# A hybrid decoder layer on one core: weight casts, sums and matmuls chained in stream order, and half a hidden block deferred

## The chip, the cores and the metric

The kernel runs on one core of one Trainium2 chip. The metric is the device time of one execution in microseconds (us); lower is better. A profile is one execution recorded by the hardware profiler.

## The reference

One decoder layer in fp32, 256 tokens, width 2048. Batch and depth are 1. Cut to what matters:

```python
def reference(x, mem, ...):
    hn = rmsnorm(x, norm_mix_w)
    q, k, v, g_ret, xr, yr, g_a, g_b = jnp.split(hn @ w_in, offsets, axis=-1)
    ret = head_groupnorm(chunkwise_retention(rotary(q), rotary(k), v))   # 8 heads, chunks of 128
    hr = rg_lru(causal_dwconv(xr, ...), ...)                             # gated linear recurrence
    merged = (jax.nn.sigmoid(g_a) * ((jax.nn.silu(g_ret) * ret) @ w_proj_ret)
              + jax.nn.sigmoid(g_b) * ((jax.nn.gelu(yr) * hr) @ w_proj_rnn))
    h = x + merged @ w_mix_out
    h = h + memory_cross_attention(rmsnorm(h, norm_xa_w), rmsnorm(mem, norm_mem_w), ...)  # 4 heads
    up = causal_dwconv(rmsnorm(h, norm_ffn_w) @ ffn_w_up, ...)           # 2048 -> 2 x 5632, 3 taps
    gate, val = jnp.split(up, 2, axis=-1)
    h = h + (jax.nn.silu(gate) * val) @ ffn_w_down                       # 5632 -> 2048
    return rmsnorm(h, final_norm_w)
```

## The kernel before, in words

All large weights come as one stream of pieces of 1 MB, `raw`, 128 partitions by 4 k-tiles by 512 columns (`wall`). Every piece is one unit of work. `prefetch(n)` keeps `AHEAD` = 2 units ready: SyncE's queue loads the piece (some pieces are added to an earlier one by an accumulating transfer in GpSimd's queue), ScalarE casts it to a short mantissa (`hi`, L284), and VectorE takes the difference (`lo = raw - hi`, L285). TensorE then multiplies with both, the activations being split the same way, so that fp32 accuracy is kept: in `gemm_t` (L349) the weight is the stationary operand, a 512-wide matmul with `hi` and a 256-wide one with `lo`; in `upper_n` (L360, L361) and `lower_n` (L367) the activations are stationary. There are `RAW_BUFS` = 5 buffers for pieces and `PART_BUFS` = 3 each for `hi` and `lo`.

Products whose two column blocks are done together (`pair_products`) use seven instead of eight block products for the first eight k-tiles, with sums of weight blocks, and plain products for k-tiles 8 to 15. `PAIR_UNITS` gives the order of the eleven units: products q1 to q7 with 12 matmuls each and four plain units p with 24 each. A weight block A, B or C stays in its buffer: after q5 VectorE adds B to A's buffer (L292), after q6 it adds C (L290), and the accumulating transfer changes B and A.

`later(n, fn)` puts a step off until n more units are done. The other work (rotary, scores and decay of the retention, group norm, recurrence, cross-attention, convolution) is written between the units like this, and the order on each engine comes from a list scheduler that works with priorities; results of a pair are read with raised priority. So the program's order need not be the order on an engine.

The FFN goes in three parts of 4, 4 and 3 hidden blocks of 512 (`FF_PARTS`). For each block `conv_up` makes the gate and the value half, two accumulators of two tiles each (`pr` = 0, 1): the product, `scaled` (two VectorE steps per accumulator, L541 and L672), a convolution step on ScalarE (L1187) and four taps on VectorE (L1189). Then come tanh (L1257), two VectorE steps (L1258, L1259) and the split into high and low (L551 on ScalarE, L552 on VectorE). `hid` holds eight such tile pairs per part. In parts 0 and 1 the down projection goes as two paired products (`pair_add`, which adds to the residual rows, L427); in the last part, as plain ones (`down`).

In the retention, a head's scores (`sc`) are multiplied by the decay matrix into a tile `pret` (L768, L769), then split into `ps` (L771 on ScalarE, L772 on VectorE). After the fourth head of a group `normalise` computes a reciprocal root (L610 on GpSimd, L796) and scales. In the value pair, results are copied and subtracted into `o` (L454, L460, L470).

Of the kernel before, what the change touches and what calls it, by code (L numbers as in the profile page):

```python
# [13 lines left out]
ALU = mybir.AluOpType  # L14
# [16 lines left out]
RAW_BUFS = 5  # L31
# [63 lines left out]
def residual_plan(w):  # L95
# [8 lines left out]
    ("p", None, (1, 8)),  # L104
    ("q3", "B", ("new", 1, 1)),
    ("p", None, (1, 12)),
# [3 lines left out]
    ("p", None, (0, 8)),  # L110
    ("q7", "B", ("add", 0, 1)),
    ("q4", "A", ("sum",)),
    ("p", None, (0, 12)),
]

def entry_units(e):

    w, row, nk, cols = e[0], e[1], e[2], e[3:5]
    if len(cols) == 1:
        return [("p", None, "new", (w, tuple(row + (k + i) * P for i in range(KC)), cols[0])) for k in range(0, nk, KC)]  # L120
    out = []
    for kind, slot, a in PAIR_UNITS:
        if kind == "p":
# [29 lines left out]
def hybrid_layer(  # L153
# [20 lines left out]
    bp = ctx.enter_context(tc.tile_pool(name="bp", bufs=25))  # L174
# [58 lines left out]
    held, after = {}, []  # L233
# [12 lines left out]
    def prefetch(n):  # L246
        while len(ahead) < n and taken[0] < len(stream):
# [30 lines left out]
            for a, b in pieces:  # L278
                if taken[0] <= 4:
                    xs[2 * (taken[0] - 1) + (b - 1) // KH]  # L280
                if first and b <= KH:
                    dve.tensor_copy(hi[:, a:b], raw[:, a:b])  # L282
                else:
                    act.copy(hi[:, a:b], raw[:, a:b])  # L284
                dve.tensor_tensor(  # L285
                    out=lo[:, a:b], in0=raw[:, a:b], in1=hi[:, a:b].bitcast(F32), op=ALU.subtract
                )
            if after:
                to, by = (held[i] for i in after.pop())
                dve.tensor_tensor(out=to, in0=to, in1=by, op=ALU.add)  # L290
            if kind == "q5":
                dve.tensor_tensor(out=raw, in0=raw, in1=held["B"], op=ALU.add)  # L292
# [33 lines left out]
    def gemm_t(w, row, st, nk, col):  # L326
# [4 lines left out]
        for k0, parts in chunks(nk, w, row, col):  # L331
# [9 lines left out]
            for i, run in enumerate(runs):  # L341
                for t, pr, kk, j in run:
# [6 lines left out]
                    pe.matmul(  # L349
                        a, part, sx, start=k == 0 and t == 0, stop=k == nk - 1 and t == 0, skip_group_check=True  # L350
                    )
# [4 lines left out]
    def upper_n(o, ops, parts, start):  # L356

        for kk, (h, l) in enumerate(ops):
            hi = parts[kk // KH][0][:, kk % KH, :]
            pe.matmul(o, h, hi, start=start and kk == 0, stop=False, skip_group_check=True)  # L360
            pe.matmul(o, l, hi, start=False, stop=False, skip_group_check=True)  # L361

    def lower_n(o, ops, parts, stop):

        for kk, (h, _) in enumerate(ops):
            lo = parts[kk // KH][1][:, kk % KH, :]
            pe.matmul(o, h, lo, start=False, stop=stop and kk == KC - 1, skip_group_check=True)  # L367
# [15 lines left out]
    def pair_products(w, row, st, ss, c0, c1, out):  # L383
# [7 lines left out]
        begun, plain = set(), 0  # L391
# [10 lines left out]
        for kind, parts in units(*e):  # L402
            if kind == "p":
                k0 = 8 + 4 * (plain % 2)
                run(
                    (((r, "r"), (w_, "w")), ((y, "y"), (u, "u")))[plain // 2],
                    [
                        [halves(st[(k0 + k) // 2], k % 2, slice(tt * P, (tt + 1) * P)) for k in range(KC)]
                        for tt in range(2)
                    ],  # L410
                    parts,
                )
                plain += 1
# [7 lines left out]
            with tc.high_priority(URGENT):  # L421
                out(f"p{plain}" if kind == "p" else kind, x, z, yu, rw)

    def pair_add(w, row, st, ss, c0, c1, h0, h1):
# [4 lines left out]
        def out(kind, x, z, yu, rw):  # L429
# [10 lines left out]
            elif kind == "p4":  # L440
# [4 lines left out]
    def pair_out(w, st, ss, c0, r=None):  # L445
# [30 lines left out]
        def out(kind, x, z, yu, rw):  # L476
# [11 lines left out]
            elif kind == "p4":  # L488
# [267 lines left out]
    def retain(g, qr, kr, vs, dec, gates):  # L756
# [4 lines left out]
        def scores(hh):  # L761
# [5 lines left out]
            pr_ = tp.tile([P, 384], F32, tag="pret", bufs=2, name=nm("pret"))  # L767
# [7 lines left out]
        def values(hh, phi, plo):  # L775
# [405 lines left out]
    def conv_up(c0, b, dst):  # L1181
        for pr, a in enumerate(gemm_t("ffn_w_up", 0, h2s, NT, c0 + b * BW)):
            z = scaled(a, "uz")
            for j in range(2):
                t = c0 // P + 4 * b + 2 * pr + j
                y = dst[:, 2 * pr + j, :]
                act.activation(y, z[:, j, :], AF.Identity, scale=pf[:, 2, t : t + 1], bias=pf[:, 3, t : t + 1])  # L1187
                for s in range(1, 3):
                    dve.scalar_tensor_tensor(  # L1189
                        out=y[:, s:S], in0=z[:, j, 0 : S - s], scalar=pf[:, 2 - s, t : t + 1], in1=y[:, s:S],  # L1190
                        op0=ALU.mult, op1=ALU.add,
                    )
# [52 lines left out]

    b0 = 0
    for part, nb_ in enumerate(FF_PARTS):
        final = part == len(FF_PARTS) - 1
        hid, hid_sums = [], []
        for b in range(b0, b0 + nb_):  # L1250
            gt, vl = big([P, 4, S], s="fg"), big([P, 4, S], s="fv")
            conv_up(0, b, gt)
            conv_up(FF, b, vl)
            for pr in range(2):
                cs = slice(2 * pr, 2 * pr + 2)
                th, o = tmp("ft"), tmp("fo")
                act.activation(th, gt[:, cs, :], AF.Tanh, scale=0.5)  # L1257
                dve.scalar_tensor_tensor(out=o, in0=th, scalar=1.0, in1=gt[:, cs, :], op0=ALU.add, op1=ALU.mult)  # L1258
                dve.tensor_tensor(out=o, in0=o, in1=vl[:, cs, :], op=ALU.mult)  # L1259
                hid.append(split_pair(o, 0.5))  # L1260
                if nb_ == 4 and len(hid_sums) < KC:
                    hid_sums.append(sums(o, 0.5))
# [51 lines left out]
```

## Time and profile before

| | |
|---|---|
| time, median of 3 runs | 2009.64 us (2009.12 to 2011.54) |
| the profiled execution | 2011.54 us, span 2009.8 us, mean granted clock 0.998 |
| TensorE busy | 1989.9 us, 99% of the span |
| VectorE busy | 1585.2 us, 79% |
| ScalarE busy | 1158.7 us, 58% |
| data moved | 430.97 MB, mean 214 GB/s |

Engines are PE (TensorE), PEld (its weight loads), DVE (VectorE), ACT (ScalarE), POOL (GpSimd) and SP (SyncE, which issues most transfers). In the timeline a line gives the start, the duration, the engine, the line of the kernel, the operation and its tiles; in square brackets stands the idle time just before, and what ended it. Matmuls are pipelined: the distance from start to start tells what one costs, not its duration.

### The profile page before, as it was taken

To read this page: it belongs to the slowest core of one execution; us is meant where nothing else is said; L and a number is where in the kernel's file an instruction comes from. 1 tells how busy PE (TensorE), PEld (TensorE's weight loads), DVE (VectorE), ACT (ScalarE), POOL (GpSimd) and SP (SyncE) were. 2 spreads that over 40 slices of the span, in tenths; PEclk is the share of its full clock that TensorE was granted. 3 is DMA by queue.
4 is the path that set the end of the run, shared out by engine and by line. 5 is a ranking of instruction groups with operands and counts; after the bars stand their busy time and mean duration, and the time that the engine had idled before them with its cause. 6 is when DMAs were issued, how large, how long until landed. Compare 5 with 4: busy or idle time off the path is not lost.

```text
span 2009.8 us, 24882 instructions
## 1 busy us (share of the span) xinstructions
PE 1989.9 (99%) x10072; PEld 1691.7 (84%) x10072; DVE 1585.2 (79%) x1588; ACT 1158.7 (58%) x1167; POOL 43.0 (2%) x52
## 2 busy tenths in 40 slices
PE   9999999999999999999999999999999999999998
PEld 7888888888888888888888888888878888788887
DVE  6798797889985886768888768777787787886765
ACT  6565656767665554566766556555544555544552
POOL 0000000000000000000000000000000000000000
PEclk9999999999999999999999999999999999999999
DMA  9664674655977775877886647655567555584552
GB/s 369 237 226 140 229 245 176 210 202 145 295 245 246 214 246 189 262 249 234 267 246 204 254 130 223 233 187 196 182 197 238 194 189 188 170 264 173 200 198 84
DMA packets 76003, 430.97 MB, mean 214 GB/s; under 512 B 8304, under 2 KB 13040, under 8 KB 28144
## 3 DMA queue, kind: packets, MB, share of 16 engines
q1 hardware_dynamic: 68608, 384.81, 52.2%
q0 software_dynamic: 5760, 41.95, 11.5%
q10 hardware_dynamic: 1520, 2.63, 0.4%
q8 instruction: 79, 1.29, 0.2%
q14 instruction: 36, 0.29, 0.0%
HBM read 418.87 MB, written 10.49 MB: 214 GB/s over the span
## 4 chain that ended last, share of the span: by engine, by line
PE 91%; DVE 5%; DMA 1%; issue 1%; ACT 1%; POOL 0%; SPq 0%; POOLq 0%; ACTq 0%; DVEq 0%
PE acc L349 37%; PE acc L360 17%; PE acc L361 17%; PE acc L367 16%; DVE lo L285 2%; PE sm L518 2%; DMA raw<-in_wall 1%; PE sm L530 1%; ACT hi L284 1%; PE acc L518 1%; PE sm L892 1%; DVE raw L292 0%; DVE fv L1189 0%; DVE tb L718 0%; DMA xt<-in_mem_t 0%
## 5 line engine op out<-in xcount | busy, mean ns | idle before, releaser
L285 DVE TENSOR_TENSOR lo<-raw,hi 128x2048 fp32r<-128x2048 f32 (+1 forms) x420 | 950.7, 2268 | 299.1 <-ACT hi L284 286.0
L284 ACT CAST hi<-raw 128x2048 fp32r<-128x2048 f32 (+1 forms) x418 | 792.8, 1902 | 624.1 <-PE acc L361 292.6
L360 PE MATMUL acc<-hi,s 128*128 128x512 f32 x1336 | 523.3, 392 | 4.3 <-ACT hi L284 3.9
L361 PE MATMUL acc<-hi,s 128*128 128x512 f32 x1336 | 520.7, 390 | 0.2 <-DVE s L575 0.2
L349 PE MATMUL acc<-s,hi 128*128 128x512 f32 x2176 | 518.0, 391 | 2.2 <-DVE hi L282 1.1
L349 PEld LDWEIGHTS acc<-s,hi 128*128 128x128 f32 x2176 | 401.9, 188 | 82.1 <-ACT hi L284 1.8
L367 PE MATMUL acc<-lo,s 128*128 128x512 f32 x1336 | 340.1, 392 | 0.1
L360 PEld LDWEIGHTS acc<-hi,s 128*128 128x128 f32 x1336 | 251.0, 188 | 58.0 <-ACT hi L284 5.2
L367 PEld LDWEIGHTS acc<-lo,s 128*128 128x128 f32 x1336 | 250.1, 188 | 53.6 <-DVE lo L285 0.5
L361 PEld LDWEIGHTS acc<-hi,s 128*128 128x128 f32 x1336 | 251.0, 188 | 52.2 <-DVE s L575 1.0
L349 PEld LDWEIGHTS acc<-s,lo 128*128 128x128 f32 x2176 | 277.0, 191 | 9.9 <-DVE lo L285 1.3
L349 PE MATMUL acc<-s,lo 128*128 128x256 f32 x2176 | 282.9, 283 | 0.5 <-DVE lo L285 0.5
L360 PE MATMUL acc<-hi,ss 128*128 128x512 f32 x320 | 127.2, 397 | 3.6 <-DVE o L470 1.7
L361 PE MATMUL acc<-hi,ss 128*128 128x512 f32 x320 | 125.5, 392 | 0.0
L367 PE MATMUL acc<-lo,ss 128*128 128x512 f32 x320 | 86.0, 390 | 0.0
L540 ACT COPY c<-acc 128x512 f32<-128x512 f32 x68 | 39.2, 578 | 75.2 <-PE acc L349 74.9
L360 PEld LDWEIGHTS acc<-hi,ss 128*128 128x128 f32 x320 | 60.6, 189 | 18.2 <-ACT hi L284 2.5
L361 PEld LDWEIGHTS acc<-hi,ss 128*128 128x128 f32 x320 | 60.6, 189 | 12.2
L367 PEld LDWEIGHTS acc<-lo,ss 128*128 128x128 f32 x320 | 60.0, 188 | 12.7
L265 POOL DMA_DIRECT2D raw<-in_wall x40 | 35.2, 879 | 1574.2 <-DVE lo L285 845.2
L427 DVE TENSOR_TENSOR nat<-nat,acc 128x512 f32<-128x512 f32 (+1 forms) x49 | 44.0, 910 | 6.7 <-PE acc L367 6.7
L290 DVE TENSOR_TENSOR raw<-raw,raw 128x2048 f32<-128x2048 f32 x20 | 45.8, 2288 | 0.4
(233 smaller groups left out, 1242.6 us busy)
## 6 DMA issues: line engine op xcount, KB each, us to landing
raw<-in_wall SPq DMA_DIRECT2D x333, 1024.0 KB, 4.9
raw<-in_wall POOLq DMA_DIRECT2D x40, 1024.0 KB, 8.0
xt<-in_x_t SPq DMA_DIRECT2D x11, 256.0 KB, 7.0
raw<-in_wall SPq DMA_DIRECT2D x5, 512.0 KB, 8.5
nat<-in_x ACTq DMA_DIRECT2D x4, 512.0 KB, 9.8
ret<-hd SPq DMA_DIRECT2D x8, 256.0 KB, 5.1
rnn<-rn SPq DMA_DIRECT2D x8, 256.0 KB, 3.1
kt<-ret SPq DMA_DIRECT2D x8, 256.0 KB, 5.6
```

The lines of the kernel that those rows point to most:

```text
L265: pool.dma_start(out=raw, in_=src, accum_op=ALU.add)
L284: act.copy(hi[:, a:b], raw[:, a:b])
L285: dve.tensor_tensor(out=lo[:, a:b], in0=raw[:, a:b], in1=hi[:, a:b].bitcast(F32), op=ALU.subtract)
L290: dve.tensor_tensor(out=to, in0=to, in1=by, op=ALU.add)
L349: pe.matmul(a, part, sx, start=k == 0 and t == 0, stop=k == nk - 1 and t == 0, skip_group_check=True)
L360: pe.matmul(o, h, hi, start=start and kk == 0, stop=False, skip_group_check=True)
L361: pe.matmul(o, l, hi, start=False, stop=False, skip_group_check=True)
L367: pe.matmul(o, h, lo, start=False, stop=stop and kk == KC - 1, skip_group_check=True)
L427: dve.tensor_tensor(out=o, in0=o, in1=i, op=op)
L518: pe.matmul(o, a, b, start=start and i == 0, stop=stop and i == 2, skip_group_check=True)
L530: pe.transpose(t[:, j, tt * P : (tt + 1) * P], rows[:, tt, k + j * P : k + (j + 1) * P], ident)
L540: act.copy(c, a[:, :, S:BW])
```

## The change

Five things change.

1. `in_turn` ties instructions of one queue to one another by scheduling edges without a semaphore: ScalarE's casts of weights in the stream's order, VectorE's casts, differences and weight sums, and TensorE's matmuls with weights. Each stays behind the one before it in the program.
2. The plain units are named and reordered: k-tiles 8 to 11 of both column blocks come first (p0, p1), k-tiles 12 to 15 later (p2, p3, the 8th and 11th unit). Before, the second plain unit (the 4th unit) took k-tiles 12 to 15.
3. The reciprocal root of the group norm is a step of its own, one unit after the fourth head, and `normalise` comes one unit later; `pret` shares the tag `tmp`.
4. In parts 0 and 1 of the FFN the value half of the last block is put off: convolution, gating and split of `pr` = 0 come after the first unit of the down projection, those of `pr` = 1 after the third.
5. The residual rows lie in memory (`fkept`) during the up projections: 12 stores and 12 loads of 512 KB in SyncE's queue. There is one more buffer for pieces (6) and one large buffer less (24).

The numbers of instructions on TensorE, ScalarE, VectorE and GpSimd stay as they were.

```diff
-RAW_BUFS = 5
+RAW_BUFS = 6
...
 PAIR_UNITS = [
     ("q1", "A", ("new", 0, 0)),
-    ("p", None, (1, 8)),
+    ("p0", None, (1, 8)),
     ("q3", "B", ("new", 1, 1)),
-    ("p", None, (1, 12)),
+    ("p1", None, (0, 8)),
     ("q5", "A", ("add", 0, 1)),
     ("q2", "C", ("new", 1, 0)),
     ("q6", "A", ("sum",)),
-    ("p", None, (0, 8)),
+    ("p2", None, (1, 12)),
     ("q7", "B", ("add", 0, 1)),
     ("q4", "A", ("sum",)),
-    ("p", None, (0, 12)),
+    ("p3", None, (0, 12)),
 ]
...
-    bp = ctx.enter_context(tc.tile_pool(name="bp", bufs=25))
+    bp = ctx.enter_context(tc.tile_pool(name="bp", bufs=24))
...
+    def in_turn(queue, ins):
+
+        if queue in last:
+            info = mybir.DependencyInfo(mybir.DependencyClass.NoSync, mybir.DependencyReason.DATA)
+            tc.add_manual_dep(ins.ins, last[queue].ins.name, info, reason="in turn")
+        last[queue] = ins
+        return ins
...
-                    act.copy(hi[:, a:b], raw[:, a:b])
-                dve.tensor_tensor(
+                    in_turn("a", act.copy(hi[:, a:b], raw[:, a:b]))
+                in_turn("d", dve.tensor_tensor(
                     out=lo[:, a:b], in0=raw[:, a:b], in1=hi[:, a:b].bitcast(F32), op=ALU.subtract
-                )
+                ))
...
-                    pe.matmul(
+                    in_turn("p", pe.matmul(
                         a, part, sx, start=k == 0 and t == 0, stop=k == nk - 1 and t == 0, skip_group_check=True
-                    )
+                    ))
...
             if hh == 3:
-                later(2, normalise)
-
-        def normalise():
+                later(1, rsqrt)
+
+        def rsqrt():
             rstd = rsqrt_small(stats[:, :, 1], 8, 1.0, GN_EPS).rearrange("p (h t) -> p h t", t=2)
+            later(1, lambda: normalise(rstd))
+
+        def normalise(rstd):
...
+    def put_rows(n, bs):
+        for b in bs:
+            sp.dma_start(out=fkept[n, b], in_=hrow[b])
+
+    def get_rows(n, bs):
+        for b in bs:
+            hrow[b] = big([P, 2, BW], s="nat")
+            sp.dma_start(out=hrow[b], in_=fkept[n, b])
...
+    put_rows(0, range(4))
...
+            for pr, z in enumerate(up(0, b)):
+                conv(0, b, pr, z, gt)
+            if b + 1 == b0 + nb_:
+                later(0, lambda part=part, n=2 if paired else 4: get_rows(part % 2, range(n)))
+            for pr, z in enumerate(up(FF, b)):
+                def finish_up(b=b, pr=pr, z=z, gt=gt, vl=vl, paired=paired):
+                    conv(FF, b, pr, z, vl)
+                    hidden(gt, vl, pr, paired)
+
+                if paired and b + 1 == b0 + nb_:
+                    later(1 + 2 * pr, finish_up)
+                else:
+                    finish_up()
...
             for b in (0, 2):
+                if b == 0:
+                    later(4, lambda part=part: get_rows(part % 2, (2, 3)))
                 pair_add("ffn_w_down", b0 * BW, hid, hid_sums, b * BW, (b + 1) * BW, hrow[b], hrow[b + 1])
+                put_rows((part + 1) % 2, (b, b + 1))
```

`conv` and `hidden` hold what stood in `conv_up` and in the loop over `pr`; the weight sums, `upper_n` and `lower_n` are wrapped in `in_turn` in the same way ("d" and "p").

More of the change, by code (lines that the diff above doesn't have):

```diff
@@ L366, in lower_n @@
             lo = parts[kk // KH][1][:, kk % KH, :]
[L367 removed]
+            in_turn("p", pe.matmul(o, h, lo, start=False, stop=stop and kk == KC - 1, skip_group_check=True))
     def gemm_n(w, row, st, nk, col):
@@ L402, in pair_products @@
         for kind, parts in units(*e):
[L403 to L413, printed above, removed]
+            if kind in rows:
+                k0, *to = rows[kind]
+                ops = [
+                    [halves(st[(k0 + k) // 2], k % 2, slice(tt * P, (tt + 1) * P)) for k in range(KC)]
+                    for tt in range(2)
+                ]
+                run(to, ops, parts)
             else:
```

72 lines of the change are left out of this document (37 added, 35 removed).

## The prediction

> **What bounds the kernel now.** I read the page's busy times and costliest groups first, then the table of stretches by 100 us, then the list of what TensorE waits for (us in total, times, longest), and last the timeline of the few places where that list has an entry.
>
> ```profile
> span 2009.8 us, 24882 instructions
> PE 1989.9 (99%) x10072; PEld 1691.7 (84%) x10072; DVE 1585.2 (79%) x1588; ACT 1158.7 (58%) x1167; POOL 43.0 (2%) x52
> L285 DVE TENSOR_TENSOR lo<-raw,hi 128x2048 fp32r<-128x2048 f32 (+1 forms) x420 | 950.7, 2268 | 299.1 <-ACT hi L284 286.0
> L284 ACT CAST hi<-raw 128x2048 fp32r<-128x2048 f32 (+1 forms) x418 | 792.8, 1902 | 624.1 <-PE acc L361 292.6
> ```
>
> ```profile
> core 0: us, PE busy (x) PEld busy (x) DVE busy (x) ACT busy (x) POOL busy (x), PEclk, DMA share, GB/s
> 0.00:100.00 100.00, 96.24 (x481) 81.52 (x482) 70.86 (x94) 61.49 (x79) 1.95 (x6) 1.00 0.83 304
> 100.00:200.00 100.00, 99.11 (x490) 82.51 (x489) 88.54 (x100) 58.22 (x55) 4.46 (x4) 1.00 0.58 182
> ...
> 400.00:500.00 100.00, 100.00 (x541) 87.18 (x541) 87.83 (x99) 72.79 (x92) 1.80 (x2) 1.00 0.54 174
> ...
> 1400.00:1500.00 100.00, 97.22 (x494) 82.54 (x493) 80.62 (x79) 53.52 (x48) 2.66 (x3) 0.98 0.58 184
> ...
> 1700.00:1800.00 100.00, 97.28 (x449) 80.46 (x449) 85.35 (x66) 51.63 (x37) 3.48 (x4) 1.00 0.69 210
> ```
>
> ```profile
> PE acc L360 <- ACT hi L284: 5.5, 4, 2.0
> PE acc L360 <- DVE o L470: 1.7, 3, 1.0
> ```
>
> TensorE is busy for 1989.9 of 2009.8 us, so everything outside it is worth at most some 20 us of idling plus what matmuls lose at a lower clock. The change adds and removes no matmul, cast, difference or sum; it only changes their order. What can move is therefore in a few places: the start (96.24 of 100), the retention stages around 100 to 300 us, and the two stretches at 1400 and 1700 (97.22, 97.28). The stretch at 400 stands for the rest: TensorE 100.00, though VectorE is 87.83 busy.
>
> The profiled run took 2011.54 us, 1.7 outside its span, and is the slowest of the three; the median is 2009.64. The sum below is made against 2011.54 and carried over at the end.
>
> **The change part by part. The gated FFN's two paired down-projections** (parts 0 and 1).
>
> TensorE's timeline (start, duration, then the idle time before it and what ended it):
>
> ```profile
> 1451.76 0.40 PE L360 MATMUL acc<-hi,s 128*128 128x512 f32 x1
> ...
> 1471.44 0.39 PE L360 MATMUL acc<-hi,s 128*128 128x512 f32 x1
> ...
> 1472.58 0.39 PE L361 MATMUL acc<-hi,s 128*128 128x512 f32 x1
> ...
> 1474.68 0.50 PE L360 MATMUL acc<-hi,ss 128*128 128x512 f32 x1 [0.81 <-ACT hi L284]
> ...
> 1485.13 0.50 PE L360 MATMUL acc<-hi,s 128*128 128x512 f32 x1 [1.96 <-ACT hi L284]
> ...
> 1497.75 0.39 PE L360 MATMUL acc<-hi,s 128*128 128x512 f32 x1
> ...
> 1716.49 0.40 PE L360 MATMUL acc<-hi,s 128*128 128x512 f32 x1
> ...
> 1749.84 0.50 PE L360 MATMUL acc<-hi,s 128*128 128x512 f32 x1 [1.93 <-ACT hi L284]
> ...
> 1760.88 0.39 PE L360 MATMUL acc<-hi,s 128*128 128x512 f32 x1
> ```
>
> The same timeline for VectorE, one stretch of 5 us, and two rows of the page's DMA part (the last number is the median from issue to landing):
>
> ```profile
> 1458.54 1.66 DVE L1189 SCALAR_TENSOR_TENSOR fv<-uz,pf,fv 128x255 f32<-128x255 f32 x4
> ...
> 1460.12 0.69 DVE L1259 TENSOR_TENSOR fo<-fo,fv 128x512 f32<-128x512 f32 x1
> ...
> 1463.12 2.28 DVE L285 TENSOR_TENSOR lo<-raw,hi 128x2048 fp32r<-128x2048 f32 x1
> ...
> 1470.33 2.29 DVE L292 TENSOR_TENSOR raw<-raw,raw 128x2048 f32<-128x2048 f32 x1
> ```
>
> ```profile
> 1485.00:1490.00 5.00, 4.87 (x14) 3.90 (x15) 5.00 (x5) 1.88 (x2) 0.00 (x0) 0.66 0.89 316
> ```
>
> ```profile
> raw<-in_wall POOLq DMA_DIRECT2D x40, 1024.0 KB, 8.0
> ...
> nat<-hkept SPq DMA_DIRECT2D x4, 512.0 KB, 6.9
> ```
>
> Five matmuls in a row start from 1471.44 to 1472.58, so one takes 0.228 us. A pair of column blocks is seven products of 12 matmuls (2.7 us each) and four plain units of 24 (5.45 us), 180 in all: 40.9 us. The first pair after part 0 runs from 1451.76 to 1497.75, 46.0 us, and the one after part 1 from 1716.49 to 1760.88, 44.4 us. So they lose 5.1 and 3.5 us.
>
> Why: before, the fourth unit, 10.9 us after the start, reads the last two hidden tiles. VectorE owes until then two groups of convolution and gating (per group about 1.66 for four taps, and five steps of about 0.69: 5.1, so 10.2 for both), one block addition (0.69, like L1259) and two differences (2.28 each): 15.5 us of work against 10.9. All that stands behind them comes late too: the weight sum L292, due for the accumulating transfer, ends only at 1472.62. The transfer lands 8.0 us after its issue, and ScalarE then casts q7's piece and the one behind it (1.9 each): 1472.6 + 8.0 + 3.8 = 1484.4, with some 0.7 for the issue the 1485.13 at which the 1.96 us of idling end.
>
> After the change that hidden half is first read by p2, the eighth unit, 24.5 us after the start (five products of 12 and two units of 24 come before it: 108 matmuls). The groups are split over units 1 and 3 and VectorE takes weights in stream order. I walk VectorE's queue from the start T of the pair: the difference for q3 ends at T+3.5, the second block's scaling, one addition and the difference for p1 by 7.6, the first group's taps, q5's difference and the sum L302 by about 15.0, q2's difference 17.9 (first read at 20.9), the second group's taps 19.5, q6's difference 22.4 (read at 23.6), p2's 25.3 (read at 28.1). None is late. What is late is the last split: on ScalarE the cast for q7 stands ahead of it, and that waits for the accumulating transfer: 15.0 + 0.7 + 8.0 + 1.9 = 25.6, then the split's own cast and difference (0.5 to 0.7 each) until about 26.9. TensorE wants it at T+26.3, after p2's first eight matmuls. I take 0.6 us of waiting per pair, with 0 and 3.5 as ends (3.5 if the transfer lands 3 us later). So the first pair gains 4.5, the second 2.9.
>
> About 1.6 of the first gain is clock: right after the 1.96 us of idling the granted clock is 0.66 between 1485 and 1490, while the second pair with its 1.93 us keeps its clock, and that is the difference between 5.1 and 3.5. [...]
>
> The price of the deferral: the residual rows go to memory and back, 12 stores and 12 loads of 512 KB in the SP queue, and free four large buffers. Such a load lands in 6.9 us. The first two are issued while up-projections still run; the other two wait in SP's queue for the second group (about T+23), and behind them stand only weight pieces for the next pair, first read after T+40. The stores wait for the additions after a pair, with pieces behind them that are needed some 30 us later, and one more weight buffer gives slack. I cost this at nothing; without that cover one load's 6.9 us would show per pair.
>
> **The start.**
>
> ```profile
> 5.79 0.70 PE L349 MATMUL acc<-s,hi 128*128 128x512 f32 x2 [1.09 <-DVE hi L282]
> ...
> 10.13 0.73 PE L349 MATMUL acc<-s,hi 128*128 128x512 f32 x2 [1.04 <-ACT hi L284]
> 11.39 0.39 PE L349 MATMUL acc<-s,lo 128*128 128x256 f32 x1 [0.53 <-DVE lo L285]
> 11.62 0.39 PE L349 MATMUL acc<-s,hi 128*128 128x512 f32 x1
> ...
> 11.96 0.40 PE L349 MATMUL acc<-s,hi 128*128 128x512 f32 x1
> ...
> 13.85 0.85 PE L349 MATMUL acc<-s,hi 128*128 128x512 f32 x3
> ```
>
> Before, TensorE did the first two k-tiles for both accumulators while the third piece of weights came (cast at 10.13, difference at 11.39), and then only 14 matmuls until 13.85. The edges now force the program's order: all four k-tiles of the first accumulator, then the second. Of 16 matmuls that used to run early 8 now stand behind 11.39, plus one 512-wide one from 10.13. A 512- and a 256-wide one together take 0.34 (11.62 to 11.96): 4 x 0.34 + 0.23 = 1.6 us later at 13.85. From there on TensorE ran without a wait in that stage, so nothing absorbs it: loss 1.6.
>
> **The first retention output pair.**
>
> ```profile
> 97.16 0.39 PE L360 MATMUL acc<-hi,s 128*128 128x512 f32 x1
> ...
> 139.78 0.39 PE L349 MATMUL acc<-s,hi 128*128 128x512 f32 x1
> ```
>
> ```profile
> 116.36 6.68 DVE L285 TENSOR_TENSOR lo<-raw,hi 128x2048 fp32r<-128x2048 f32 x3
> ...
> 149.20 0.56 DVE L772 TENSOR_TENSOR ps<-pret,ps 128x384 fp32r<-128x384 f32 x1 [0.58 <-ACT ps L771]
> ```
>
> It runs from 97.16 to 139.78: 42.6, so 1.7 over 40.9. After, two heads' scores, which stood near 149, come forward. Twelve score matmuls stand right behind q3 and wait for the rotated queries' difference (about 1.0 us). The heads' four VectorE steps, which pass back and forth with ScalarE, stand between the differences that ran as one block from 116.36, and q6's cast behind them on ScalarE: by my walk it ends 1.9 us late, and its difference 0.3 after that. New waits 3.2, old ones 1.7 gone, since the transfer behind them then comes in time: loss 1.5. Ends: 0 if the scores fit beside the plain units, 3.2 if the old waits stay too.
>
> **The retention value pair.**
>
> ```profile
> 201.31 0.68 DVE L470 TENSOR_TENSOR o<-o,acc 128x512 f32<-128x512 f32 x1
> ```
>
> ```profile
> 202.05 0.50 PE L360 MATMUL acc<-hi,ss 128*128 128x512 f32 x1 [1.05 <-DVE o L470]
> ```
>
> TensorE waits 1.05 us for L470, which stood behind the group norm's steps; the reciprocal root is now a step of its own, one unit earlier, and L470 comes in time. Gain 1.1, with the slow first matmul; ends 0 and 1.7 (all waits for L470).
>
> **The other pairs and stages.** Their matmul order is nearly the same; weight sums swap with a neighbouring difference, and four scans and the gate product come forward around 500 us. The stretch at 400 shows TensorE at 100.00. Ends: no cost, and two waits like that at 202.05 (2.1); I take 0.5.
>
> Sum: +1.6 +1.5 -1.1 -4.5 -2.9 +0.5 = -4.9, so 2006.6 against the profiled 2011.54. The other runs are some 2 us faster than the profiled one; if the low clock at 1485 is its own (1.6), the change is -3.3 from 2009.64, so 2006.3. Forecast 2006.4, for the median.
>
> **The rivals.** *The losses don't come* (both early walks wrong, residues zero): -1.5 -1.2 from the forecast: 2003.7. For it: VectorE idles near 149. *The clock closes in the start.* Before, 16 matmuls filled 5.79 to 9.09 (10.13 less 1.04); 8 end by about 7.5, and then TensorE has one matmul until 11.39. If that lowers the clock as at 1485, another 1.6 goes: 2008.0. For it: 0.66 after 1.96 of idling; against it: 1.93 at 1749.84 without. [...] *The late half eats the gain*: the accumulating transfer lands 3 us later, so each down pair waits 3.6. Against a run without the low clock, where the two lost 3.5 each: 7.2 - 7.0 + 2.5 (the other terms) = +2.7, so 2012.3. *Slower*: the accumulating transfer queues behind a residual load (6.9 more). The last split then ends at T+33.8, a wait of 7.5, and with the clock's 1.6 each pair loses 9.1: 18.2 - 7.0 + 2.5 = +13.7, so 2023.3. It decides from a wait of 4.3 per pair (2 x 4.3 - 7.0 + 2.5 = 4.1), a landing of 11.7 us instead of 8.0. For it: the transfers are busy for 0.89 of 1485 to 1490 already; against it: the late loads are issued only when that transfer has nearly landed. *The edges do nothing* where the order was already so: the second retention output pair keeps its waits, which the sum has at zero.
>
> **How the numbers follow.** A measurement of this kernel can tell about 0.2%, 4 us: below 2005.6 is faster, above 2013.7 slower. Chances: forecast 0.50 (its own range 2003 to 2010 lies on both sides of 2005.6: 0.30 faster, 0.20 same); losses absent 0.10 (faster); clock at the start 0.14 (0.02 faster, 0.12 same); gain eaten 0.13 (same); slower 0.13. Together faster 0.42, same 0.45, slower 0.13. The range 2002.5 to 2013 leaves out the slower case and a small part of the absent losses.
>
> **What would show it.** In the profile after: the rows of 1400 and 1700 rise to over 99 and the waits on `hi` shrink to under 1 us each; the 0:100 row falls to about 94.7; one new wait on a difference or cast between 108 and 124; no wait for L470 near 202. Wrong would be waits over 2 us in the two down pairs, a new wait on a transfer anywhere, or any 100 us stretch now at 100.00 falling below 99.

## The result: slower, 2025.45 us, ratio 1.0070

The changed kernel takes 2025.45 us (median of 4 runs, 2023.03 to 2028.34) against 2010.51 for the kernel before in the same runs. The ratio is 1.0070, 95% interval 1.0057 to 1.0083, so about 14 us slower. The forecast was 2006.4, with a range from 2002.5 to 2013.

The profiled run of the changed kernel took 2023.03 us with a span of 2021.3. All lines of the kernel behind the weight order are now some 10 higher: L349 became L359, L360, L361 and L367 became L370, L371 and L377, L284 and L285 became L294 and L295. In an experiment they shift once more, by the lines that its edit adds. From the page, and from the table of stretches:

```profile
span 2021.3 us, 24954 instructions
PE 1994.1 (99%) x10072; PEld 1695.8 (84%) x10072; DVE 1583.7 (78%) x1588; ACT 1158.9 (57%) x1167; POOL 47.1 (2%) x52
```

```profile
core 0: us, PE busy (x) PEld busy (x) DVE busy (x) ACT busy (x) POOL busy (x), PEclk, DMA share, GB/s
0.00:100.00 100.00, 95.71 (x470) 81.06 (x471) 68.25 (x93) 59.44 (x76) 1.95 (x6) 0.98 0.84 307
100.00:200.00 100.00, 93.05 (x454) 78.28 (x453) 82.17 (x92) 53.85 (x50) 2.62 (x3) 0.95 0.49 162
...
1400.00:1500.00 100.00, 99.26 (x525) 85.06 (x524) 80.44 (x84) 55.52 (x50) 1.79 (x2) 1.00 0.62 207
...
1700.00:1800.00 100.00, 99.02 (x468) 82.53 (x467) 85.34 (x68) 54.93 (x40) 3.49 (x4) 1.00 0.73 234
...
1900.00:2000.00 100.00, 96.57 (x495) 82.49 (x494) 68.27 (x72) 47.61 (x50) 0.00 (x0) 0.98 0.42 158
```

The forecast's gain is there: 1400 rose from 97.22 to 99.26 and 1700 from 97.28 to 99.02. But 100 to 200 fell from 99.11 to 93.05, with a clock of 0.95, and 1900 to 2000 is at 96.57. Before it was full:

```profile
1900.00:2000.00 100.00, 100.00 (x547) 87.04 (x546) 67.25 (x76) 45.10 (x47) 0.57 (x1) 1.00 0.40 148
```

What TensorE waits for after the change (us in total, times, longest):

```profile
PE acc L370 <- DVE v L572: 5.8, 1, 5.8
PE acc L370 <- ACT s L559: 2.2, 2, 1.8
PE acc L371 <- DVE s L560: 2.1, 3, 1.6
PE acc L370 <- DVE o L478: 1.3, 2, 1.0
```

To compare places including lost clock, I take the distance from each matmul's start to the next, less what that shape takes at full clock (0.227 us for 512 columns and 0.120 for 256, the medians of both traces; for 128 I set 0.100, where the median is 0.108), and add it up by stretch, from one profiled run of each kernel. The stretches left out have within 0.7 us the same in all of them, and the columns are the experiments of the next section:

| stretch | before | changed | no edges on TensorE (a1) | old unit order, all edges (a2) | both taken back (a3) | no edges at all, old order (a4) | edges on TensorE alone, on the kernel before (b1) | as a4, no deferral (b3) |
|---|---|---|---|---|---|---|---|---|
| 0 to 100 | 6.1 | 8.6 | 7.3 | 10.3 | 5.7 | 6.0 | 9.3 | 6.1 |
| 100 to 200 | 2.8 | 11.0 | 5.5 | 2.7 | 2.7 | 3.0 | 3.0 | 2.8 |
| 200 to 300 | 2.7 | 1.3 | 1.3 | 1.4 | 1.3 | 1.2 | 2.7 | 1.3 |
| 300 to 900 | 7.7 | 10.3 | 9.3 | 12.0 | 9.4 | 7.7 | 8.6 | 7.7 |
| 900 to 1000 | 1.2 | 0.5 | 2.4 | 5.5 | 1.2 | 3.4 | 3.1 | 1.4 |
| 1400 to 1500 | 5.2 | 1.7 | 1.3 | 1.8 | 1.3 | 1.3 | 4.9 | 3.6 |
| 1700 to 1800 | 3.5 | 1.8 | 1.3 | 1.5 | 0.9 | 0.9 | 6.3 | 5.0 |
| 1900 to 2000 | 0.3 | 5.7 | 0.4 | 6.5 | 0.4 | 0.3 | 6.5 | 0.4 |
| whole span | 32.8 | 43.9 | 31.9 | 45.4 | 25.8 | 27.1 | 47.6 | 32.1 |

The changed kernel loses 11.2 us more than before by this measure; its span is 11.5 longer. Three places make 16.0 of losses: the first retention output pair (8.2), the last part of the FFN (5.3), the start (2.5). The down pairs gain 5.2 (3.5 and 1.7), the value pair 1.4; small losses between 300 and 900 add 2.6, among them new waits of 0.87 and 1.01 us near 318 and 520, where TensorE had been at 100.00.

**The first retention output pair.** TensorE's timeline, one stretch, and VectorE's:

```profile
110.49 0.63 PE L526 MATMUL sm<-s,s 128*128 128x256 f32 x4
112.01 1.12 PE L526 MATMUL sm<-s,s 128*128 128x256 f32 x8 [0.89 <-DVE s L557]
118.94 0.79 PE L370 MATMUL acc<-hi,s 128*128 128x512 f32 x1 [5.81 <-DVE v L572]
119.53 0.63 PE L371 MATMUL acc<-hi,s 128*128 128x512 f32 x1
119.95 0.63 PE L370 MATMUL acc<-hi,s 128*128 128x512 f32 x1
```

```profile
115.00:120.00 5.00, 1.06 (x3) 0.87 (x4) 5.00 (x5) 0.69 (x1) 0.87 (x1) 0.50 0.11 48
```

```profile
115.28 0.74 DVE L572 SCALAR_TENSOR_TENSOR v<-acc,ro,v 128x512 fp32r<-128x512 f32 x1
115.94 2.28 DVE L302 TENSOR_TENSOR raw<-raw,raw 128x2048 f32<-128x2048 f32 x1
118.14 0.74 DVE L572 SCALAR_TENSOR_TENSOR v<-acc,ro,v 128x512 fp32r<-128x512 f32 x1
```

The scores wait 0.89, as forecast. Then p1, the fourth unit, waits 5.81 until the second L572 has read the value product out of its accumulator (118.14 to 118.88); after that the matmuls start 0.43 apart instead of 0.23, at a clock of 0.50. There are three accumulators for all weight products. In the old order the fourth unit goes on in the accumulator that the second has begun; the third is first written by q2, the sixth. The new p1 writes it as the fourth. By the trace's record the clock falls to 0.50 at 114.72 already, 1.6 us into this wait; what the traces show of that stands in the last section.

**The last part's down projection.** TensorE and VectorE after the change:

```profile
1952.59 0.39 PE L371 MATMUL acc<-hi,s 128*128 128x512 f32 x1
1954.77 0.50 PE L370 MATMUL acc<-hi,s 128*128 128x512 f32 x1 [1.79 <-ACT s L559]
1956.91 0.50 PE L371 MATMUL acc<-hi,s 128*128 128x512 f32 x1 [1.64 <-DVE s L560]
1957.25 0.40 PE L370 MATMUL acc<-hi,s 128*128 128x512 f32 x1
...
1957.94 0.63 PE L371 MATMUL acc<-hi,s 128*128 128x512 f32 x1
```

```profile
1953.97 2.28 DVE L295 TENSOR_TENSOR lo<-raw,hi 128x2048 fp32r<-128x2048 f32 x1
1956.17 0.68 DVE L560 SCALAR_TENSOR_TENSOR s<-fo,s 128x512 fp32r<-128x512 f32 x1
```

And before, at the same point of the program:

```profile
1948.10 2.29 DVE L285 TENSOR_TENSOR lo<-raw,hi 128x2048 fp32r<-128x2048 f32 x1
1950.30 0.69 DVE L552 SCALAR_TENSOR_TENSOR s<-fo,s 128x512 fp32r<-128x512 f32 x1
```

```profile
1950.85 0.40 PE L361 MATMUL acc<-hi,s 128*128 128x512 f32 x1
1951.08 0.39 PE L367 MATMUL acc<-lo,s 128*128 128x512 f32 x1
```

VectorE does the same steps in the same order in both, and the split of the last hidden tiles ends behind a difference in both. Before, TensorE went on with matmuls that don't need it (L361 and L367 mix between 1948 and 1957) and had no gap. With the edges it stands at the first one that does.

**The start.**

```profile
9.74 0.50 PE L359 MATMUL acc<-s,hi 128*128 128x512 f32 x1 [0.94 <-ACT hi L294]
11.00 0.39 PE L359 MATMUL acc<-s,lo 128*128 128x256 f32 x1 [0.76 <-DVE lo L295]
```

```profile
10.00:15.00 5.00, 4.24 (x17) 3.49 (x17) 4.56 (x7) 4.42 (x8) 0.00 (x0) 0.73 1.03 413
```

Eight matmuls now stand behind the third piece, as forecast, and the clock falls to 0.73 behind the wait, which the forecast had as a rival.

### The profile page after: what moved, and what is told of

It is laid out like the page before. It is cut to its first block, busy times and chain, and to the rows that moved or that the text cites. A ratio compares the mean times of both kernels' runs of the same rounds, so it can differ in the third digit from the quotient of the medians.

```text
span 2021.3 us, 24954 instructions
## 1 busy us (share of the span) xinstructions
PE 1994.1 (99%) x10072; PEld 1695.8 (84%) x10072; DVE 1583.7 (78%) x1588; ACT 1158.9 (57%) x1167; POOL 47.1 (2%) x52
## 3 DMA queue, kind: packets, MB, share of 16 engines
q0 software_dynamic: 5760, 41.95, 11.2%
## 4 chain that ended last, share of the span: by engine, by line
PE 89%; DVE 6%; DMA 2%; issue 1%; ACT 1%; SPq 0%; POOLq 0%; ACTq 0%; DVEq 0%
PE acc L359 37%; PE acc L370 16%; PE acc L371 16%; PE acc L377 16%; DVE lo L295 3%; PE sm L526 2%; DMA raw<-in_wall 1%; PE sm L538 1%; ACT hi L294 1%; PE acc L526 1%; PE sm L903 1%; DVE raw L302 0%; DVE raw L300 0%; DVE fv L1201 0%; DVE tb L726 0%
## 5 line engine op out<-in xcount | busy, mean ns | idle before, releaser
L295 DVE TENSOR_TENSOR lo<-raw,hi 128x2048 fp32r<-128x2048 f32 (+1 forms) x420 | 951.7, 2267 | 311.7 <-ACT hi L294 306.3
L294 ACT CAST hi<-raw 128x2048 fp32r<-128x2048 f32 (+1 forms) x418 | 793.7, 1902 | 626.1 <-PE acc L371 279.1
L370 PE MATMUL acc<-hi,s 128*128 128x512 f32 x1336 | 525.3, 393 | 8.3 <-DVE v L572 5.8
L371 PE MATMUL acc<-hi,s 128*128 128x512 f32 x1336 | 523.5, 392 | 2.1 <-DVE s L560 2.1
L359 PE MATMUL acc<-s,hi 128*128 128x512 f32 x2176 | 519.2, 391 | 3.0 <-DVE hi L292 1.1
L359 PEld LDWEIGHTS acc<-s,hi 128*128 128x128 f32 x2176 | 402.8, 188 | 83.4 <-issue 2.7
L377 PE MATMUL acc<-lo,s 128*128 128x512 f32 x1336 | 340.2, 392 | 0.0
L370 PEld LDWEIGHTS acc<-hi,s 128*128 128x128 f32 x1336 | 252.4, 189 | 61.2 <-DVE v L572 5.9
L371 PEld LDWEIGHTS acc<-hi,s 128*128 128x128 f32 x1336 | 252.3, 189 | 54.6 <-DVE s L560 3.0
L377 PEld LDWEIGHTS acc<-lo,s 128*128 128x128 f32 x1336 | 250.4, 188 | 53.5
L359 PEld LDWEIGHTS acc<-s,lo 128*128 128x128 f32 x2176 | 277.5, 192 | 10.1 <-DVE lo L295 2.0
L359 PE MATMUL acc<-s,lo 128*128 128x256 f32 x2176 | 283.5, 284 | 1.1 <-DVE lo L295 1.1
L370 PE MATMUL acc<-hi,ss 128*128 128x512 f32 x320 | 126.4, 395 | 2.5 <-DVE o L478 1.3
L371 PE MATMUL acc<-hi,ss 128*128 128x512 f32 x320 | 124.8, 390 | 0.0
L377 PE MATMUL acc<-lo,ss 128*128 128x512 f32 x320 | 86.0, 390 | 0.0
L370 PEld LDWEIGHTS acc<-hi,ss 128*128 128x128 f32 x320 | 60.1, 188 | 17.1 <-DVE nat L435 1.6
L377 PEld LDWEIGHTS acc<-lo,ss 128*128 128x128 f32 x320 | 60.0, 188 | 12.7
L371 PEld LDWEIGHTS acc<-hi,ss 128*128 128x128 f32 x320 | 60.1, 188 | 12.1
L435 DVE TENSOR_TENSOR nat<-nat,acc 128x512 f32<-128x512 f32 (+1 forms) x49 | 43.9, 908 | 4.2 <-PE acc L377 4.2
L302 DVE TENSOR_TENSOR raw<-raw,raw 128x2048 f32<-128x2048 f32 x20 | 45.7, 2285 | 0.2
```

The lines of the kernel that those rows point to most:

```text
L294: in_turn("a", act.copy(hi[:, a:b], raw[:, a:b]))
L295: in_turn("d", dve.tensor_tensor(out=lo[:, a:b], in0=raw[:, a:b], in1=hi[:, a:b].bitcast(F32), op=ALU.subtract))
L302: in_turn("d", dve.tensor_tensor(out=raw, in0=raw, in1=held["B"], op=ALU.add))
L359: in_turn("p", pe.matmul(a, part, sx, start=k == 0 and t == 0, stop=k == nk - 1 and t == 0, skip_group_check=True))
L370: in_turn("p", pe.matmul(o, h, hi, start=start and kk == 0, stop=False, skip_group_check=True))
L371: in_turn("p", pe.matmul(o, l, hi, start=False, stop=False, skip_group_check=True))
```

## The experiments

Two theories stood at first. A: two causes, each by itself, the edges on TensorE (start, last part) and the new unit order (the wait at 119). B: one cause, TensorE's edges, since without them it could have passed the wait at 119 as well. C was a third for the details, the edges on VectorE and ScalarE: those on VectorE make the order that hurts, or both make the gain in the down pairs.

**Edges on TensorE out (a1).** `in_turn` returns at once for the queue "p":

```diff
     def in_turn(queue, ins):
+        if queue not in 'ad':
+            return ins
```

> The changed kernel without the edges between TensorE's matmuls; the edges on ScalarE and VectorE, the new unit order, the deferral and the residual rows in memory stay. Theory A (two separate causes): TensorE's edges cost the start (2.5 us) and the last down projection (5.3 us), since TensorE can no longer take a later matmul while an operand is late; the long wait of 5.8 us in the first retention output pair comes from the new unit order instead, which needs the third accumulator at the fourth unit. Then the waits at 10 and at 1955 us go, the one at 119 stays in the main, and the time is 8 us below the changed kernel: about 2016. Theory B (one cause): the edges between matmuls alone cost all of it, the wait at 119 too: about 2008.

Measured: 2009.14 us, ratio 0.9990 (0.9981 to 1.0000). A's 2016 is out; B's 2008 is right. The wait at 119 is gone too. TensorE passes it:

```profile
110.75 1.12 PE L528 MATMUL sm<-s,s 128*128 128x256 f32 x8 [0.90 <-DVE s L559]
113.06 0.50 PE L372 MATMUL acc<-hi,ss 128*128 128x512 f32 x1 [1.20 <-ACT o L464]
```

Behind the scores TensorE takes q5 (operands `hi,ss`) and leaves p1 for later. What is left there is 2.7 us over before (5.5 against 2.8), about what the forecast had for this pair with its bounds (1.5, up to 3.2).

**Old unit order outside the down projection, all edges kept (a2).**

```diff
+    late = w == "ffn_w_down"
+    swap = {"p1": ("p2", None, (1, 12)), "p2": ("p1", None, (0, 8))}
-    for kind, slot, a in PAIR_UNITS:
+    for kind, slot, a in [u if late else swap.get(u[0], u) for u in PAIR_UNITS]:
```

> The changed kernel, all edges kept, but the old order of the plain units in every pair outside the FFN's down projection. Theory A: the first retention output pair has no wait above 1 us near 119 and loses no clock there, 7 to 8 us; the waits at the start and at 1955 stay: about 2016. Theory B: the wait at 119 stays, within 2 us of the changed kernel, about 2024.

Measured: 2021.38 us, ratio 1.0053 (1.0037 to 1.0069). The wait at 119 goes, as A said (100 to 200 is at 2.7), but A's 2016 is missed: the whole gains only some 4 us by the medians, and the intervals overlap. In the profiled run other waits come where there were none. The largest part is 5.0 us more in 900 to 1000, where TensorE stands before the split of a tile of normalised activations.

```profile
926.08 0.50 PE L373 MATMUL acc<-hi,s 128*128 128x512 f32 x1 [1.33 <-DVE s L585]
929.07 0.80 PE L373 MATMUL acc<-hi,s 128*128 128x512 f32 x1 [1.58 <-DVE s L585]
```

So the order mainly decides what is late; that it costs this much comes from the edges.

**Both taken back (a3).**

> No edges between matmuls and the old unit order outside the down projection. Theory A: both losses go, the gain in the two down pairs (5.2 us by the traces) stays: 2006 to 2009. Theory B: the same as without TensorE's edges alone.

Measured: 2005.52 us, ratio 0.9974 (0.9965 to 0.9983): faster than the kernel before, and just under the 2006 to 2009 that A gave. Without TensorE's edges alone it was 0.9990, so by the ratios the old order outside the down projection is worth 0.16% more; the two intervals just touch, and the table has the same 2.8 us in 100 to 200. B, which gave it nothing, is wrong in this: where TensorE is free the new order still costs a little. What is left there with the new order are the waits of 0.90 and 1.20 us above and matmuls 0.43 apart behind them, from 114.18 to 115.89, where a1 has 0.23 from 118.01 on.

**All edges out (a4).** As a3, and `in_turn` returns for every queue.

> As the kernel with both taken back, and the edges on ScalarE and VectorE gone too, so that only the deferral, the rows in memory, the step of the reciprocal root and the new order in the down pairs are left. Theory A: ScalarE's and VectorE's edges cost and bring little, within 3 us of the kernel with them, 2005 to 2010. Rival C: those edges make the gain in the down pairs (casts in time for the transfers); without them waits of 1 to 2 us come back near 1485 and 1750, 3 to 4 us more.

Measured: 2003.58 us, ratio 0.9961 (0.9945 to 0.9978). That is just under A's 2005 to 2010 and within 3 us of a3. C is out: the stretches at 1400 and 1700 stay at 1.3 and 0.9 without the edges on ScalarE and VectorE.

```profile
1400.00:1500.00 100.00, 99.52 (x512) 84.74 (x511) 83.51 (x80) 55.62 (x48) 2.66 (x3) 1.00 0.66 211
...
1700.00:1800.00 100.00, 99.77 (x454) 82.46 (x453) 87.02 (x65) 53.11 (x36) 3.49 (x4) 1.00 0.76 244
```

**TensorE's edges alone on the kernel before (b1).** Only the matmuls of `gemm_t`, `upper_n` and `lower_n` in `in_turn("p", ...)`, nothing else of the change.

> The kernel before with one part of the change alone: the edges that keep TensorE's weight matmuls in the program's order. Theory B (these edges are the cause): the start loses 2.5 us and the last down projection 5 us here too, and the two paired down projections, where TensorE went on with other units while it waited, lose more than before: 2018 to 2026. Theory A (the edges cost only together with the new unit order): within 3 us of the kernel before.

Measured: 2025.66 us, ratio 1.0075 (1.0060 to 1.0090). B again. This one part costs as much as the whole change. Its waits:

```profile
PE acc L369 <- DVE s L560: 3.8, 3, 1.6
PE acc L368 <- ACT s L559: 3.3, 3, 1.8
PE acc L368 <- DVE nat L435: 2.7, 2, 2.2
PE acc L368 <- DVE o L478: 2.3, 3, 1.0
PE acc L369 <- DVE s L583: 2.0, 2, 1.6
```

The splits of late hidden tiles (L559, L560), the read of an accumulator before its reuse (L435, L478) and the split of normalised activations (L583): every late operand now stops TensorE.

**TensorE's edges kept, the other two queues free (b2).**

> The changed kernel without the edges on ScalarE and VectorE; those on TensorE stay. Theory B: the start, the wait near 119 and that near 1955 stay, so 2020 to 2026. Rival C: it is VectorE's edges that put the weight sum in front of the value split for which TensorE waits at 119; then that wait falls by 2 to 4 us and its lost clock with it, and the time to 2015 to 2019.

Measured: 2022.56 us, ratio 1.0049 (1.0032 to 1.0066). The wait for the value split is 5.8 us as before, and C is out here as well. Against the changed kernel (1.0057 to 1.0083) the intervals overlap.

**No deferral (b3).** As a4, but `finish_up` is called at once:

```diff
-                if paired and b + 1 == b0 + nb_:
+                if False:
                     later(1 + 2 * pr, finish_up)
```

> The kernel without any edges, with the old unit order outside the down projection, and with the last block's value half no longer put off; residual rows in memory and the new order in the down pairs stay. If the new order alone gives TensorE the time (the hidden half is due at the eighth unit anyway), it stays within 1 us of the kernel with the deferral, 2003 to 2005; if the deferral is what spreads VectorE's work, 2 to 4 us come back in the stretches at 1400 and 1700.

Measured: 2011.14 us, ratio 1.0004 (0.9995 to 1.0013). The new order in the down pairs brings nothing by itself: the waits are where they were.

```profile
1473.37 0.50 PE L374 MATMUL acc<-hi,ss 128*128 128x512 f32 x1 [0.98 <-ACT hi L298]
1483.76 0.50 PE L374 MATMUL acc<-hi,s 128*128 128x512 f32 x1 [1.93 <-ACT hi L298]
```

The deferral is worth the 7 us between this and a4 (0.35 to 0.43%), more than the 2 to 4 expected; in the table the two stretches at 1400 and 1700 lose 6.4 more. Without it VectorE still does both groups ahead of the differences and the sum (L306), whichever unit needs the hidden half. Its timeline without the deferral, and with it in the changed kernel, whose pair starts 11 us later in the trace:

```profile
1458.22 0.87 DVE L1205 SCALAR_TENSOR_TENSOR fv<-uz,pf,fv 128x254 f32<-128x254 f32 x2
...
1464.62 4.49 DVE L299 TENSOR_TENSOR lo<-raw,hi 128x2048 fp32r<-128x2048 f32 x2
1469.02 2.29 DVE L306 TENSOR_TENSOR raw<-raw,raw 128x2048 f32<-128x2048 f32 x1
```

```profile
1475.23 2.28 DVE L302 TENSOR_TENSOR raw<-raw,raw 128x2048 f32<-128x2048 f32 x1
...
1480.23 1.66 DVE L1201 SCALAR_TENSOR_TENSOR fv<-uz,pf,fv 128x255 f32<-128x255 f32 x4
```

With the deferral the second group's taps (1480.23) come behind the sum, without it ahead of it. In the program the two groups stand behind the second and the fourth unit of the down projection, not behind the first and the third, since `later` is called here when the up projection's last unit is already counted. The old order's fourth unit reads the tiles that the second group makes, so the deferral as written needs the new order, and no run has it with the old one: the 7 us are what the deferral brings on top of an order that allows it. The rows in memory cost nothing that shows: this kernel has them too, is at before's time, and no wait of TensorE there is for a transfer of rows.

**The reciprocal root back in one step (b4).** As a4, with `later(2, rsqrt)` and the scaling in the same step.

> The kernel without any edges, with the old unit order outside the down projection, and with the reciprocal root again in one step with the scaling, two units after the fourth head. Expected: the wait of 1.05 us in the retention value pair near 202 comes back, 1.1 to 1.4 us slower, 2005.

Measured: 2005.70 us, as expected, ratio 0.9977 (0.9968 to 0.9986); a4 had 0.9961 and, run again, 0.9969. The wait comes back at 203.86 (1.04 us of idling, 1.2 by the table's measure), and the stretch at 200 loses 2.7 instead of 1.2. The intervals overlap, so the size rests on the trace.

**Three places free (c3).** The changed kernel, with TensorE's edges left out only in the first product, the first retention output pair and the last part's down projection:

```diff
+    free = {plan[0], [e for e in plan if len(e) == 5][0]}
+    free.update(e for e in plan if e[0] == "ffn_w_down" and len(e) == 4)
...
+        if queue == "p" and plan[gemms[0] - 1] in free:
+            return ins
```

> The changed kernel, with TensorE's edges left out in three places only: the first product, the first retention output pair and the last part's down projection. If the edges cost only where an operand is late, and these are the places, about 2.5 (less its own 0.5), 5 to 6 and 5.5 us come back and the rest stays: 2009 to 2012, like the changed kernel without any edges on TensorE (2009.1). If the edges cost a little everywhere, it stays above 2015.

Measured: 2010.90 us, ratio 1.0001 (0.9992 to 1.0010), as expected. Freedom in three of the many products gives back nearly all that a1 does (0.9990).

**Edges on VectorE alone, on ScalarE alone, and a4 once more (c1, c2).**

> The kernel with the deferral, the old order outside the down pairs and no edges on TensorE or ScalarE; those on VectorE are in. If the edges on VectorE bring nothing, within 1.5 us of the kernel without any (2003.6); the wait of 2.1 us near 918 there may move.

> The same with the edges on ScalarE alone. If they bring nothing, within 1.5 us of the kernel without any (2003.6). If the casts in order keep the 2.1 us wait near 918 away, 2001.5.

> The kernel with the deferral, the rows in memory, the step of the reciprocal root and the new order in the down pairs alone, once more beside the three others: 2003 to 2006.

Measured, on one chip: 0.9983 (0.9974 to 0.9992), 0.9972 (0.9961 to 0.9982), and 0.9969 (0.9958 to 0.9980) without any. ScalarE's edges do nothing that can be told; VectorE's bring nothing, and by the mean they cost 0.14%, with intervals that just overlap; that is 2.8 us, outside the expected 1.5. The hope that the casts in order keep the wait near 918 away did not show: a4 itself has it once with 1.86 us of idling and once with 0.62, so it moves from run to run.

**The values read first (d1, d2).** What TensorE waits for at 119 was read from one row so far. In the changed kernel, edges and order kept, two lines change places, so that the value accumulators are read ahead of the rotary steps:

```diff
-                turned.append(rotated(a))
                 vs.append(split_rows(v, rs0))
+                turned.append(rotated(a))
```

> The changed kernel, all edges and the new unit order kept, with one swap in the program: the split of the values out of their accumulator (two steps each on ScalarE and VectorE) is written ahead of the rotary steps, not behind them. If TensorE waits near 119 because p1, now the fourth unit, needs an accumulator which that split still reads, the wait of 5.8 us and its lost clock go: 6 to 8 us below the changed kernel, 2016 to 2019, with the start and the wait near 1955 as they were. If it waits for something else there (the two heads' scores, an operand), at least 3 us of it stay: above 2020.

Measured: 2019.77 us, ratio 1.0038 (1.0025 to 1.0051). The second L572 now ends at 111.2 and the wait is gone; p1 begins without a gap at 111.29:

```profile
110.48 0.75 DVE L572 SCALAR_TENSOR_TENSOR v<-acc,ro,v 128x512 fp32r<-128x512 f32 x1
```

```profile
111.29 0.50 PE L370 MATMUL acc<-hi,s 128*128 128x512 f32 x1
```

The stretch from 100 to 200 falls from 11.0 to 3.6 by the measure of the table. The time fell by 6 us, and lies just over the expected 2016 to 2019, as 900 to 1000 lost 1.9 more. So the wait was the accumulator's. With it the scheduler also left the two heads' scores later in the program: presumably they had been put there because it had nothing else to put in front of p1; that was not tried by itself.

> The same swap in the kernel with the deferral and without edges, where the old order asks for that accumulator at the sixth unit only and 0.3 us are lost near 116: 0 to 0.6 us faster than it (2003.6 to 2005.1), not to be told from it.

Measured: 2006.15 us, ratio 0.9975 (0.9966 to 0.9985): not to be told from a4, as expected.

The version to keep is a4: the deferral, the rows in memory, the reciprocal root's own step, the new unit order in the down pairs alone, and no edges. It had 0.9961 (0.9945 to 0.9978) and 0.9969 (0.9958 to 0.9980), 6 to 8 us under the kernel before; a3 and c2 are not to be told from it.

## Why the prediction was wrong, step by step

The forecast's sum was -4.9 us; by the table the changed kernel loses 11.2 more than before. Of the 16.1 between, 6.7 are the first retention output pair and 5.3 the last part of the FFN; 2.6 come from 300 to 900, 2.2 from the down pairs and 0.9 from the start, and the rest takes 1.6 off. One of the forecast's own signs of being wrong showed: two stretches that had been at 100.00 fell below 99, 1900 to 2000 (96.57) and 500 to 600 (98.68).

**The FFN's down pairs: mechanism right, size somewhat too large.** Forecast gains were 4.5 and 2.9; the traces show 3.5 and 1.7, and the rows of 1400 and 1700 rise over 99 as forecast. Two things are left in each pair, here the first:

```profile
1489.28 0.50 PE L371 MATMUL acc<-hi,s 128*128 128x512 f32 x1 [0.22 <-DVE s L560]
1494.28 0.50 PE L370 MATMUL acc<-hi,ss 128*128 128x512 f32 x1 [0.38 <-DVE nat L435]
```

The last split costs 0.8 us over the normal distance (forecast 0.6), and a residual addition that must read an accumulator before its reuse (L435) costs 0.5, which the walk had at nothing. The sum of the walk is confirmed: the forecast had L302 end at T+15.0, and it ends 14.7 us after the pair's first matmul, which starts at 1462.84. The accumulating transfer and the rows in memory did no harm: the rivals "gain eaten" and "slower" through a transfer did not happen. What the walk did not tell apart is order and deferral: b3 shows that the order without the deferral brings nothing, and the deferral without that order was not run.

**The start: mechanism right, and a rival came true.** Of the 1.6 us from eight matmuls moved and the further 1.6 from the clock, 2.5 showed in the profiled run: 1.6 from 12.28 to 15.73, where the 512-wide matmuls took 0.43 each and the clock was 0.50, and 0.9 from the order. The clock's part was not in the sum but a rival with a chance of 0.14.

**The first retention output pair: the step that failed.** The forecast walked VectorE's and ScalarE's queues for late operands, and asked of p1 only whether its weights and activations are there. It never asked when the accumulator that p1 opens is free. That read (L572) stood behind the rotary steps and a weight sum, so the term was not 1.5 but 8.2, of which 5.8 idle time and the rest the wait for the scores and the clock.

**The other pairs and stages: the other step that failed.** The forecast put 0.5 on all the rest, because their order is nearly the same and TensorE was at 100.00 there. The last part of the FFN was among them and lost 5.3. A TensorE at 100.00 did not mean that its operands were in time. It meant that the scheduler had laid other matmuls in front of the late ones. There the order did change: the edges alone cost 15 us (b1), and freedom in three places gives 14 us back (c3). In the down pairs the forecast had even seen TensorE go on with other units before, but it took the edges' price only from the start.

**The value pair: right.** Forecast 1.1, shown 1.4 in the trace.

**A slip that changed nothing.** The rival in which the losses don't come, "both early walks wrong", takes only 1.5 (the retention pair) and 1.2 (the residues) off the forecast. If the other early walk is the start's, its 1.6 belongs there too, and the rival would have been at 2002.1.

## What to carry to other kernels

Before an engine is held to program order, list what it does now while an operand is late: a full engine may be full because it goes around waits, and holding it shows every one of them. When the order of units is changed, check for each moved unit not only its inputs but the accumulator it opens, and who reads that last. Putting off work that a stage does not need yet, in an order of units that asks for it late, and without forcing any engine's order, gave nearly all of the gain here.

## What was not expected of the hardware

Here waits cost more than their length. After 5.81 us of idling the granted clock was 0.50, and matmuls started 0.43 apart until the end of the next 5 us; after 1.79 and 1.64 us with a single matmul between them the matmuls from 1957.25 to 1957.94 still started 0.23 apart, at the full rate, and then the clock fell (0.63 us for the one at 1957.94, 0.43 apart from there). In the start the same happened after 0.94 and 0.76 us with one matmul between (0.73 from 10 to 15). So in these two places the clock fell behind short waits close together as well, 1.0 and 1.3 us after the second of them had ended.

The traces' records of the clock show when. In those of before and of the changed kernel the clock changes only at points that lie whole multiples of 3.41 us apart. In before it is 0.50 from 1485.81 to 1489.22 (3.41) and from 2004.63 to the end; in the changed kernel from 12.32 to 15.73 and from 1957.92 to 1961.33 (3.41 each), from 114.72 to 124.96 (10.24) and from 2015.94 to the end. With the two spans cut every 3.41 us at these points, the time in which TensorE had no matmul in a stretch stands beside the clock of the next:

| run | stretch | without a matmul | clock of the next stretch |
|---|---|---|---|
| before | 1482.39 to 1485.81 | 1.96 | 0.50 |
| before | 1748.63 to 1752.05 | 1.21 | 1.00 |
| changed | 8.91 to 12.32 | 1.59 | 0.50 |
| changed | 111.31 to 114.72 | 2.29 | 0.50 |
| changed | 1951.09 to 1954.51 | 1.53 | 1.00 |
| changed | 1954.51 to 1957.92 | 1.90 | 0.50 |

In these two traces every stretch at full clock with 1.59 us or more without a matmul was followed by one at 0.50: the four in the table, and in each trace the one in which the matmuls end, with 2.74 and 2.86. Those with 1.53 or less were all followed by one at 1.00. In a1 less came before it: behind the waits of 0.90 and 1.20 us, with eight matmuls between them, the matmuls start 0.43 apart from 114.18 on. This fits what the prediction left open: the wait of 1.96 us at 1485 lay whole in one stretch, while that of 1.93 at 1749.84 was cut in two, 0.72 and 1.21. Where the stretches lie differs between the two traces (the record's first one begins at 4.42 us in before and at 5.49 in the changed kernel), so whether a wait of this length costs clock is, by my estimate, partly chance.

With the edges on TensorE alone (b1) the start fares no better (9.3 in the table, against 8.6 in the changed kernel), although the table of stretches gives its first 100 us a clock of 1.00. From 10 to 15 it has 13 matmuls, where before has 21 at 1.00 and the changed kernel 17 at 0.73. A 1.00 there need not be the clock: in the changed kernel's trace the record begins at 5.49, and ahead of it the view gives 1.00 from 0 to 5, where 128-wide matmuls (L228) start 0.21 apart against the median of 0.108. That b1 ran at half rate there is my estimate from these numbers.
